# An fp32 encoder layer on one core: functions of finished products one product later in ScalarE's queue, matmuls of the means later in TensorE's

## The chip, the cores and the metric

The kernel runs on one core of one Trainium2 chip. The metric is the time on the device in microseconds (us), given as the median of several runs. One execution was also recorded by the hardware profiler, and every row shown here comes from that one.

## The reference

One layer of a two-branch encoder, in fp32, for two groups of tokens that share the weights: a prompt of 512 tokens and a sample of 1024, both 1024 wide. Cut to what matters:

```python
def conv_branch(a_val, a_glu, a_z, ...):
    h = a_val * jax.nn.sigmoid(a_glu)
    h = lax.conv_general_dilated(h, conv_w, ...) + conv_b      # depthwise, 31 taps
    h = layer_norm(h, ln_g, ln_b)
    h = jax.nn.silu(h) * jax.nn.silu(a_z)
    return h @ w_proj

def sgu_branch(u, v, b_z, ...):
    v = layer_norm(gelu(v), ln_g, ln_b)
    mixed = einsum("gpq,bnqgc->bnpgc", w_s, chunks(v)) + b_s
    return (gelu(u) * mixed * jax.nn.silu(b_z)) @ w_proj

def encoder_layer(x, c, ...):
    shift, scale, gate = split(silu(c) @ w_ada + b_ada)
    h = rms_norm(x, g_pre) * (1 + scale) + shift
    a_val, a_glu, a_z, u, v, b_z, g_a, g_b = split(h @ w_in)
    m = sigmoid(g_a) * conv_branch(...) + sigmoid(g_b) * sgu_branch(...)
    return x + gate * rms_norm(m @ w_out, g_post)
```

## The kernel before, in words

**Tiles.** Activations lie with the features on the 128 partitions and 512 tokens along a row. There are three such token tiles: the prompt `t0`, and the halves `sa` and `sb` of the sample. An fp32 product is made of three fp32r matmuls: each operand is split into a rounded part hi and a rest lo, and hi·hi, hi·lo and lo·hi are summed in a PSUM bank. A column step (128 output features of one tile, 8 blocks of 128 features deep) is 24 matmuls of 128x128 by 128x512, on the lines L449 to L451 and L472 to L474.

**Pairs.** The input projection of the sample is done two units of 128 output features at a time, by `pair` (L993), as a Strassen product: instead of eight half products it makes seven, of 12 matmuls each (L483 to L485): Xa, Ya, Xb, Zb, Xc, Zc, Xd. X, Y and Z are three banks; X runs on through four products, and between them ScalarE copies a snapshot of a bank into a work buffer (`snap`, L1014: p1 and u2 and u3 of X, s5 of Z), because the next product goes on adding to that bank. VectorE adds snapshots to banks (L1018 for C11, L1022 for C22, L1026 for C12). C11, C22, C12 and C21 are the four finished quarters, and `finish(what, st)` applies to each the function of its branch on ScalarE: `pair_func` (L1126 for quarters in a work buffer, L1131 for C21, which is still in the bank), `pair_mul` (L1148, L1153; then a product with a loaded tile on VectorE, L1158; the tile is asked for at L1142), or `pair_glu` (L1167 to L1173). There are 28 pairs in a row: 8 of glu, and 4 each of gB, um, hB, z and gA.

**What sets the order.** The program is written to the engines' queues by a planner that runs on the host. `steps` lists TensorE's steps; the loop at the end (L1715 on) goes through them. For each step `s` it writes, of the step before (`p`), `p.a1` to ScalarE; then it lets background generators (`bg`, mostly the convolution's taps at L403) put work on VectorE up to a time of the model (`fill`); then `p.d1` on VectorE, `p.a2` on ScalarE, `p.d2` on VectorE; then the matmuls of `s` on TensorE, and loads on SP's queue. Every engine works through its queue in the order in which it was written, so an instruction that waits holds up all that stand behind it on its engine.

**Means.** Two LayerNorms per token tile need a mean over the features, that is over partitions. `bcast_mean` (L324) makes hi and lo of a sum (ScalarE L320, VectorE L321), and two matmuls with a matrix of 1/1024 (L331, L332). These are not a step of their own: `pe_later(lag, cost, fn)` leaves them in a list, and the planner puts them into TensorE's queue at the first of its polls that is later than VectorE's model clock plus `lag`. `LAG` is 1.0. There are 12 such means in the program. `ln_gen` (L414) with `rstd_bcast` (L364) and `late_ln` (silu L1227, multiplication L1240, hi L1241, lo L1232) make the operand hA of a sample half from the convolution's result. The steps behind the pairs are, in this order as far as they matter here: post_B of both halves (product with sproj; VectorE takes the banks at L1292), post_A(sa) and then the output product `steps_o` of sa (ScalarE L610, VectorE L619, closing at L636 to L643), post_A(sb) (reads hA of sb; VectorE L580, L581), and steps_o of sb.

**Raw weights.** A weight block comes from HBM into `raw`, ScalarE makes hi (L247), and lo is made by VectorE (L259) or by ScalarE and a DMA of POOL (L250, L240).

Of the kernel before, what the change touches and what calls it, by code (L numbers as in the profile page):

```python
# [40 lines left out]
LAG = 1.0  # L41
# [39 lines left out]
def layer_kernel(ctx: ExitStack, tc, x_p, x_s, xt_p, xt_a, xt_b, par, w_blk, w_v, cproj, sproj, w_out, w_ada, w_gate, wsT, bs,  # L81
# [13 lines left out]
    V, S, PE, SP, GP = nc.vector, nc.scalar, nc.tensor, nc.sync, nc.gpsimd  # L95
# [107 lines left out]
    steps = []  # L203
# [70 lines left out]
    def fill(t_end, n=1000):  # L274
        while clk["dve"] < t_end and n > 0 and bg:
            i = 0
            while i < len(bg):
                r = next(bg[i], None)
                if r is None:
                    bg.pop(i)  # L280
                elif r == "wait":
                    i += 1
                else:
                    n -= 1
                    break
            else:
                clk["dve"] += 0.2
# [17 lines left out]
    def pe_later(lag, cost, fn):  # L305
        box = {}

        def go(now):
            box["b"] = fn()
            box["t"] = now  # L310
        pe_items.append((clk["dve"] + lag, cost, go))
        return box
# [12 lines left out]
    def bcast_mean(src):  # L325

        hi, lo = yield from parts(src)

        def go():
            b = bank()  # L330
            PE.matmul(b, lhsT=onemr, rhs=hi, start=True, stop=False)  # L331
            PE.matmul(b, lhsT=onemr, rhs=lo, start=False, stop=True)  # L332
            return b
        box = pe_later(LAG, 0.43, go)
        yield from ready(box)
        return box["b"]

# [651 lines left out]


    pairs = []

    def pair(src1, src2, finish):  # L993

        u1, u2 = Unit(src1, len(steps)), Unit(src2, len(steps))
        w = {}
        st = {}
# [5 lines left out]
        def prod(name, wt, i, opn, first, last, a1=None, d1=None, a2=None, need=None, act=0.6):  # L1003
            def mm():
                if first:
                    st[name] = bank()
                mm_prod(st[name], half(w[wt][0], i), half(w[wt][1], i), A[opn], first, last)
            s_ = add_step(Step(mm, a1, d1, a2, dur=PROD, need=need, act=act))
            return s_

        def snap(name, of):
            def a1():
                st[name] = wk()
                S.copy(st[name], st[of])  # L1014
            return a1
# [16 lines left out]
        mul = getattr(finish, "mul", None)  # L1032
        ask = getattr(finish, "ask", None)

        def times(*what):
            return (lambda: [mul(x) for x in what]) if mul else None

        prod("X", "a", 0, (0, 0), True, False, a1=snap("p1", "X"))
        prod("Y", "a", 1, (0, 1), True, True, d1=d_c11, a2=lambda: finish("C11", st), act=0.0)
        prod("X", "b", 0, "S2", False, False, a1=snap("u2", "X"), d1=times("C11"), need="S")  # L1040
        prod("Z", "b", 1, "S1", True, False, a1=snap("s5", "Z"))
        prod("X", "c", 0, "S3", False, False, a1=snap("u3", "X"), d1=d_c22, a2=lambda: finish("C22", st))
        prod("Z", "c", 1, "S4", False, True, d1=d_c12, a2=lambda: finish("C12", st), need="S4", act=0.0)
        steps[-1].d2 = times("C22")
        prod("X", "d", 0, (1, 1), False, True, a1=lambda: finish("C21", st),
             d1=times("C12", "C21") or (lambda: finish("end", st)))
        if ask:
            for i, what in ((1, ("C11",)), (3, ("C22",)), (4, ("C12", "C21"))):
                steps[i0 + i].extra = lambda what=what: [ask(x) for x in what]


# [654 lines left out]
    def events(s, kind):  # L1706
        for _, f in sorted(evs.pop((s, kind), []), key=lambda e: e[0]):
            f()

    for s in range(NH, n + 1):  # L1710
        p = steps[s - 1]
        st = steps[s] if s < n else None
        poll(clk["pe"])
        pe0 = clk["pe"]
        if st is not None:  # L1715
            if st.pre:
                clk["pe"] += st.pre()
            clk["pe"] += st.dur
        pe1 = clk["pe"]
        clk["act"] = max(clk["act"], pe0)  # L1720
        if p.a1:
            p.a1()
            clk["act"] += p.act
        events(s, "act")
        fill(pe0 + 0.5)
        if p.d1:
            dwait(pe0 + 0.7)
            p.d1()
        if p.a2:
            p.a2()  # L1730
            clk["act"] = max(clk["act"], clk["dve"]) + 0.6
        fill(pe1 - 1.5, 2)
        if p.d2:
            p.d2()
        events(s, "dve")
        if st is not None:
            t_need = clk["dve"]
            meet(st.need)
            if clk["dve"] > t_need and clk["dve"] > clk["pe"] - st.dur:
                clk["pe"] = clk["dve"] + st.dur  # L1740
                pe1 = clk["pe"]
            st.mm()
        load_some(s)
        if st is not None and st.extra:
            st.extra()
        fill(pe1 + 0.4)
        dwait(pe0 + 0.5)
# [68 lines left out]
```

## Time and profile before

| | us |
|---|---|
| median of 3 runs (1469.4 to 1471.98) | 1471.81 |
| the profiled execution | 1466.83 |
| its span, first to last instruction | 1464.9 |
| TensorE busy | 1432.5 (98%) |
| VectorE busy | 1129.0 (77%) |
| ScalarE busy | 742.3 (51%) |
| mean granted TensorE clock, as a share | 0.992 |

TensorE is the engine that is almost always busy. A matmul of 128x512 is listed with 0.39 us, but matmuls overlap: without a wait one starts every 0.227 us. A row of a timeline gives the start, the duration, the engine and line, the operation, what it writes and reads, and in brackets how long its engine had been idle before it and what released it. A gap between two starts on TensorE that is longer than 0.227 us is time lost to TensorE there.

### The profile page before, as it was taken

The page shows a single profiled execution, that of the slowest core. Times are in us where ns is not written, and L with a number is a line of the kernel's source. Part 1 is how long each engine was busy: PE and PEld are TensorE (multiplying, and loading weights), DVE is VectorE, ACT ScalarE, POOL GpSimd, SP SyncE. Part 2 cuts the span into 40 slices and gives each one's busy share as a digit, 9 for nine tenths or more (in the row PEclk, how much of TensorE's full clock was granted, in tenths as well). Part 3 has the DMA queues.
Part 4 walks back from the last instruction along what each step waited for, and adds up shares of the span by engine and source line. Part 5 has one row for each costly group of instructions (what it writes and reads, how often), then busy time and mean ns, then how long its engine had stood idle before and what let it go on. Part 6 is the DMA issues. An engine that isn't in the chain of part 4 may idle for free.

```text
span 1464.9 us, 17769 instructions
## 1 busy us (share of the span) xinstructions
PE 1432.5 (98%) x6332; PEld 1169.3 (80%) x6332; DVE 1129.0 (77%) x1596; ACT 742.3 (51%) x1064; POOL 186.2 (13%) x220
## 2 busy tenths in 40 slices
PE   8999999999999989999999999999999989999997
PEld 4688888888888878888888888877888867888886
DVE  6769999976356455867999898898999939587645
ACT  3532544553486454454545565555556545554442
POOL 0000111111111110011111111111111100000000
PEclk9999999999999999999999999999999999999999
DMA  9266787897999998967666878877977799878782
GB/s 342 79 215 182 198 201 166 203 256 181 279 266 244 284 263 272 281 168 201 155 158 166 209 194 242 255 211 218 256 192 191 194 307 276 265 222 237 211 269 72
DMA packets 120040, 321.68 MB, mean 220 GB/s; under 512 B 13328, under 2 KB 17040, under 8 KB 119184
## 3 DMA queue, kind: packets, MB, share of 16 engines
q1 hardware_dynamic: 88992, 229.85, 45.2%
q0 software_dynamic: 30960, 90.72, 33.7%
q8 instruction: 49, 0.80, 0.2%
q14 instruction: 39, 0.32, 0.1%
HBM read 182.10 MB, written 47.71 MB: 157 GB/s over the span
## 4 chain that ended last, share of the span: by engine, by line
PE 80%; DMA 11%; DVE 4%; issue 2%; ACT 2%; SPq 1%; DVEq 0%; ACTq 0%; POOLq 0%
PE b L451 11%; PE b L449 11%; PE b L450 11%; PE b L483 10%; PE b L484 10%; PE b L485 10%; PE b L473 4%; PE b L474 4%; PE b L472 4%; DMA lo<-raw 2%; DMA wk<-d 2%; PE b L568 1%; DMA raw<-in_w_blk_dram 1%; DMA raw<-in_sproj_dram 1%; DVE c L403 1%
## 5 line engine op out<-in xcount | busy, mean ns | idle before, releaser
L483 PE MATMUL b<-A,hi 128*128 128x512 f32 x784 | 306.8, 391 | 6.9 <-ACT wk L1014 6.9
L484 PE MATMUL b<-A,hi 128*128 128x512 f32 x784 | 305.8, 390 | 0.0
L485 PE MATMUL b<-A,lo 128*128 128x512 f32 x784 | 305.7, 390 | 0.0
L449 PE MATMUL b<-A,hi 128*128 128x512 f32 x776 | 303.7, 391 | 0.0
L451 PE MATMUL b<-A,lo 128*128 128x512 f32 x776 | 302.8, 390 | 0.2 <-DMA lo<-raw 0.2
L450 PE MATMUL b<-A,hi 128*128 128x512 f32 x776 | 302.8, 390 | 0.0
L403 DVE SCALAR_TENSOR_TENSOR c<-c,prm 128x1024 f32<-128x1024 f32 x240 | 297.3, 1278 | 0.6
L247 ACT CAST hi<-raw 128x1024 fp32r<-128x1024 f32 x145 | 152.0, 1048 | 262.4 <-DMA raw<-in_w_v_dram 61.7
L240 POOL DMA_DIRECT2D lo<-raw x131 | 113.4, 865 | 788.8 <-ACT lo L250 690.8
L483 PEld LDWEIGHTS b<-A,hi 128*128 128x128 f32 x784 | 147.6, 188 | 40.1 <-ACT wk L1014 9.7
L485 PEld LDWEIGHTS b<-A,lo 128*128 128x128 f32 x784 | 147.6, 188 | 30.5
L484 PEld LDWEIGHTS b<-A,hi 128*128 128x128 f32 x784 | 147.5, 188 | 30.6 <-DVE A L967 0.2
L451 PEld LDWEIGHTS b<-A,lo 128*128 128x128 f32 x776 | 146.1, 188 | 31.3 <-DMA lo<-raw 0.7
L449 PEld LDWEIGHTS b<-A,hi 128*128 128x128 f32 x776 | 146.1, 188 | 30.4 <-issue 0.2
L450 PEld LDWEIGHTS b<-A,hi 128*128 128x128 f32 x776 | 146.0, 188 | 30.5 <-issue 0.2
L403 DVE SCALAR_TENSOR_TENSOR S<-c,prm,S 128x512 f32<-128x512 f32 x240 | 162.6, 745 | 0.2
L473 PE MATMUL b<-lo,A 128*128 128x512 f32 x384 | 150.6, 392 | 5.0 <-DMA lo<-raw 5.0
L472 PE MATMUL b<-hi,A 128*128 128x512 f32 x384 | 150.8, 393 | 0.0
L474 PE MATMUL b<-hi,A 128*128 128x512 f32 x384 | 150.0, 391 | 0.0
L240 POOL DMA_DIRECT2D lo<-T x84 | 72.4, 862 | 456.7 <-ACT lo L1068 374.0
L1014 ACT COPY wk<-b 128x512 f32<-128x512 f32 x112 | 65.0, 585 | 121.2 <-PE b L485 117.5
L250 ACT ACTIVATE lo<-raw 128x1024 fp32r<-128x1024 f32 x103 | 108.7, 1055 | 0.0
(206 smaller groups left out, 1630.7 us busy)
## 6 DMA issues: line engine op xcount, KB each, us to landing
raw<-in_w_blk_dram SPq DMA_DIRECT2D x105, 512.0 KB, 5.6
lo<-raw POOLq DMA_DIRECT2D x103, 512.0 KB, 6.6
d<-wk SPq DMA_DIRECT2D x142, 256.0 KB, 3.7
wk<-d SPq DMA_DIRECT2D x116, 256.0 KB, 5.9
lo<-T POOLq DMA_DIRECT2D x28, 512.0 KB, 5.7
lo<-T POOLq DMA_DIRECT2D x56, 256.0 KB, 4.4
raw<-in_w_v_dram SPq DMA_DIRECT2D x24, 512.0 KB, 5.6
raw<-in_sproj_dram SPq DMA_DIRECT2D x24, 512.0 KB, 6.1
```

Source lines behind the costliest of these rows:

```text
L240: GP.dma_start(lo.bitcast(F32), src, accum_op=ALU.add)
L247: S.copy(u.hi, u.raw)
L403: lambda: V.scalar_tensor_tensor(acc, in0=win, scalar=wt, in1=acc, op0=ALU.mult, op1=ALU.add))
L449: PE.matmul(dst, lhsT=wh3[:, k, :], rhs=hi, start=(k == 0), stop=False)
L450: PE.matmul(dst, lhsT=wh3[:, k, :], rhs=lo, start=False, stop=False)
L451: PE.matmul(dst, lhsT=wl3[:, k, :], rhs=hi, start=False, stop=(k == NK - 1))
L472: PE.matmul(banks[i], lhsT=hi, rhs=wh3[:, kk, :], start=(k == 0), stop=False)
L473: PE.matmul(banks[i], lhsT=hi, rhs=wl3[:, kk, :], start=False, stop=False)
L474: PE.matmul(banks[i], lhsT=lo, rhs=wh3[:, kk, :], start=False, stop=(k == NK - 1))
L483: PE.matmul(dst, lhsT=wh3[:, k, :], rhs=hi, start=st, stop=False, skip_group_check=True)
L484: PE.matmul(dst, lhsT=wh3[:, k, :], rhs=lo, start=False, stop=False, skip_group_check=True)
L485: PE.matmul(dst, lhsT=wl3[:, k, :], rhs=hi, start=False, stop=sp, skip_group_check=True)
```

## The change

Two edits. In `bcast_mean` the matmuls of a mean are asked for `3 * LAG` after VectorE's model clock instead of `LAG`. Since they can enter only at the planner's polls (at and amid its steps), their place in TensorE's queue moves by 0, 12, 24, 36 or 48 matmuls. In `pair`, the function of C11, C22 and C12 is queued by `turn("act")` behind the snapshot that follows the next product; the multiplications (L1158) that belong to um and hB, and glu's last part, are kept for the step after and written after `fill`; and the loads that `pair_mul` asks for move from the steps 1, 3 and 4 of a pair to 2, 4 and 5. No instruction is added or removed on any engine.

```diff
@@ -331,7 +331,7 @@
             PE.matmul(b, lhsT=onemr, rhs=hi, start=True, stop=False)
             PE.matmul(b, lhsT=onemr, rhs=lo, start=False, stop=True)
             return b
-        box = pe_later(LAG, 0.43, go)
+        box = pe_later(3 * LAG, 0.43, go)
         yield from ready(box)
         return box["b"]
 
@@ -989,6 +989,12 @@
 
 
     pairs = []
+    late = {"act": [], "dve": []}
+
+    def turn(kind):
+        fns, late[kind] = late[kind], []
+        for f in fns:
+            f()
 
     def pair(src1, src2, finish):
 
@@ -1032,20 +1038,31 @@
         mul = getattr(finish, "mul", None)
         ask = getattr(finish, "ask", None)
 
-        def times(*what):
-            return (lambda: [mul(x) for x in what]) if mul else None
+        def after_next(what):
+
+            def act():
+                finish(what, st)
+                if mul:
+                    late["dve"].append(lambda: mul(what))
+            late["act"].append(act)
+
+        def c21():
+            finish("C21", st)
+            if mul:
+                late["dve"].append(lambda: mul("C21"))
+
+        def end():
+            late["dve"].append(lambda: finish("end", st))
 
         prod("X", "a", 0, (0, 0), True, False, a1=snap("p1", "X"))
-        prod("Y", "a", 1, (0, 1), True, True, d1=d_c11, a2=lambda: finish("C11", st), act=0.0)
-        prod("X", "b", 0, "S2", False, False, a1=snap("u2", "X"), d1=times("C11"), need="S")
+        prod("Y", "a", 1, (0, 1), True, True, d1=d_c11, a2=lambda: after_next("C11"), act=0.0)
+        prod("X", "b", 0, "S2", False, False, a1=snap("u2", "X"), need="S")
         prod("Z", "b", 1, "S1", True, False, a1=snap("s5", "Z"))
-        prod("X", "c", 0, "S3", False, False, a1=snap("u3", "X"), d1=d_c22, a2=lambda: finish("C22", st))
-        prod("Z", "c", 1, "S4", False, True, d1=d_c12, a2=lambda: finish("C12", st), need="S4", act=0.0)
-        steps[-1].d2 = times("C22")
-        prod("X", "d", 0, (1, 1), False, True, a1=lambda: finish("C21", st),
-             d1=times("C12", "C21") or (lambda: finish("end", st)))
+        prod("X", "c", 0, "S3", False, False, a1=snap("u3", "X"), d1=d_c22, a2=lambda: after_next("C22"))
+        prod("Z", "c", 1, "S4", False, True, d1=d_c12, a2=lambda: after_next("C12"), need="S4", act=0.0)
+        prod("X", "d", 0, (1, 1), False, True, a1=c21, d1=end)
         if ask:
-            for i, what in ((1, ("C11",)), (3, ("C22",)), (4, ("C12", "C21"))):
+            for i, what in ((2, ("C11",)), (4, ("C22",)), (5, ("C12", "C21"))):
                 steps[i0 + i].extra = lambda what=what: [ask(x) for x in what]
 
 
@@ -1718,9 +1735,11 @@
             clk["pe"] += st.dur
         pe1 = clk["pe"]
         clk["act"] = max(clk["act"], pe0)
+        muls, late["dve"] = late["dve"], []
         if p.a1:
             p.a1()
             clk["act"] += p.act
+        turn("act")
         events(s, "act")
         fill(pe0 + 0.5)
         if p.d1:
@@ -1730,6 +1749,8 @@
             p.a2()
             clk["act"] = max(clk["act"], clk["dve"]) + 0.6
         fill(pe1 - 1.5, 2)
+        for f in muls:
+            f()
         if p.d2:
             p.d2()
         events(s, "dve")
```

ScalarE's queue in a pair of gA. The names are tiles: `b` a PSUM bank, `wk` a work buffer, `raw` and `T` the weights; the first of the three copies is p1, and L1126 the sigmoid of C11. Before:

```order
L1014 COPY wk_6271<-b_6257 128x512
L1068 ACTIVATE lo_6274<-T34_6191 128x512
L1106 CAST hi_6273<-T34_6191 128x512
L1074 CAST hi_6294<-raw_6206 128x1024
L1126 ACTIVATE wk_6271<-wk_6271 128x512
L1014 COPY wk_6317<-b_6257 128x512
L1014 COPY wk_6333<-b_6319 128x512
L1068 ACTIVATE lo_6336<-T12_6301 128x1024
L1086 CAST hi_6335<-T12_6301 128x1024
```

The same place after, where L1014 is now L1020 and L1126 is L1143:

```order
L1020 COPY wk_6428<-b_6413 128x512
L1085 ACTIVATE lo_6431<-T34_6341 128x512
L1123 CAST hi_6430<-T34_6341 128x512
L1091 CAST hi_6450<-raw_6356 128x1024
L1020 COPY wk_6470<-b_6413 128x512
L1143 ACTIVATE wk_6428<-wk_6428 128x512
L1020 COPY wk_6490<-b_6475 128x512
L1085 ACTIVATE lo_6493<-T12_6454 128x1024
L1103 CAST hi_6492<-T12_6454 128x1024
```

The sigmoid of C11 stood ahead of the copies of u2 and of s5 and now stands between them. The function of C22 keeps its place behind u3, and the functions of C12 and C21 change places with each other.

TensorE's queue at the tenth mean, in the second stage of post_B. `onemr` is the matrix of 1/1024. Before, the mean stands between two column steps (`b_9753` is the column before it, `b_9798` the one after):

```order
L450 MATMUL b_9753<-A_9314,hi_9601 128x512
L451 MATMUL b_9753<-A_9314,lo_9602 128x512
L331 MATMUL b_9782<-wk_9748,onemr_90 128x512
L332 MATMUL b_9782<-wk_9749,onemr_90 128x512
L449 MATMUL b_9798<-A_9313,hi_9652 128x512
L450 MATMUL b_9798<-A_9313,hi_9652 128x512
```

After, it stands in the middle of the next column step, `b_9788`, 12 of whose matmuls are already ahead of it:

```order
L450 MATMUL b_9788<-A_9313,hi_9650 128x512
L451 MATMUL b_9788<-A_9313,lo_9651 128x512
L331 MATMUL b_9801<-wk_9748,onemr_90 128x512
L332 MATMUL b_9801<-wk_9749,onemr_90 128x512
L449 MATMUL b_9788<-A_9314,hi_9650 128x512
L450 MATMUL b_9788<-A_9314,hi_9650 128x512
```

The ninth mean, 86 matmuls earlier, stands in TensorE's queue exactly where it stood. The eleventh and twelfth stand 48 matmuls later.

VectorE's queue where steps_o of sa ends and post_A of sb begins. L1240 and L1232 (after: L1257 and L1249) are the multiplication and the lo of hA of sb, one of each for each of 8 blocks; L619 waits for the end of steps_o of sa. Before, all eight lo stand ahead of L619:

```order
L1240 TENSOR_TENSOR wk<-wk,c_10108 128x512
L1232 TENSOR_TENSOR A<-wk,A 128x512
L1240 TENSOR_TENSOR wk<-wk,c_10108 128x512
L1232 TENSOR_TENSOR A<-wk,A 128x512
L1240 TENSOR_TENSOR wk<-wk,c_10108 128x512
L1232 TENSOR_TENSOR A<-wk,A 128x512 x2
L619 TENSOR_TENSOR S<-b,G_9868 128x512 x4
L636 SCALAR_TENSOR_TENSOR ss<-q 128x4
L155 TENSOR_SCALAR r<-ss 128x4
```

After, four lo stand ahead of it:

```order
L1249 TENSOR_TENSOR A<-wk,A 128x512
L1257 TENSOR_TENSOR wk<-wk,c_10144 128x512
L1249 TENSOR_TENSOR A<-wk,A 128x512
L1257 TENSOR_TENSOR wk<-wk,c_10144 128x512
L619 TENSOR_TENSOR S<-b,G_9864 128x512 x4
L636 SCALAR_TENSOR_TENSOR ss<-q 128x4
```

and the other four behind it, behind the eleven small operations of L636 to L165 and a lo of weights (L259):

```order
L165 SCALAR_TENSOR_TENSOR r<-u,r 128x4
L259 TENSOR_TENSOR lo<-raw,hi 128x1024
L1249 TENSOR_TENSOR A<-wk,A 128x512
L1257 TENSOR_TENSOR wk<-wk,c_10144 128x512
L1249 TENSOR_TENSOR A<-wk,A 128x512
L1257 TENSOR_TENSOR wk<-wk,c_10144 128x512
L1249 TENSOR_TENSOR A<-wk,A 128x512 x2
L643 SCALAR_TENSOR_TENSOR S<-S,r 128x1024 x4
L580 TENSOR_TENSOR wk<-b,wk 128x512
```

## Rows read from the trace of the kernel before

**Rows 1.** The page, part 1: busy us (share of the span) and instructions of TensorE.
```profile
PE 1432.5 (98%) x6332; PEld 1169.3 (80%) x6332; DVE 1129.0 (77%) x1596; ACT 742.3 (51%) x1064; POOL 186.2 (13%) x220
```

**Rows 2.** Waits of TensorE (line waited for: us in total, times, longest).
```profile
PE b L483 <- ACT wk L1014: 6.9, 6, 2.1
PE b L473 <- DMA lo<-raw: 5.0, 4, 2.6
PE b L331 <- ACT wk L320: 4.1, 2, 2.6
```

**Rows 3.** Timeline of TensorE, one of the product stalls: start, duration, line, [idle before <-releaser].
```profile
1018.34 0.39 PE L485 MATMUL b<-A,lo 128*128 128x512 f32 x1
1020.53 0.50 PE L483 MATMUL b<-A,hi 128*128 128x512 f32 x1 [1.80 <-ACT wk L1014]
```

**Rows 4.** Timeline of ScalarE, the same stall.
```profile
1019.38 0.63 ACT L1148 ACTIVATE wk<-wk 128x512 f32<-128x512 f32 x1 [5.18 <-DVE wk L1018]
1019.92 1.06 ACT L1014 COPY wk<-b 128x512 f32<-128x512 f32 x2
```

**Rows 5.** Timeline of VectorE, the same product.
```profile
1013.27 0.69 DVE L1158 TENSOR_TENSOR wk<-wk 128x512 f32<-128x512 f32 x1 [1.33 <-DMA wk<-d]
...
1018.66 0.68 DVE L1018 TENSOR_TENSOR wk<-b,wk 128x512 f32<-128x512 f32 x1
```

**Rows 6.** Timeline of ScalarE, the sixth product stall.
```profile
1172.09 1.05 ACT L247 CAST hi<-raw 128x1024 fp32r<-128x1024 f32 x1 [3.45 <-DMA raw<-in_sproj_dram]
...
1174.01 0.61 ACT L1126 ACTIVATE wk<-wk 128x512 f32<-128x512 f32 x1
...
1175.55 1.06 ACT L1014 COPY wk<-b 128x512 f32<-128x512 f32 x2
```

**Rows 7.** Timeline of TensorE, the sixth product stall.
```profile
1173.66 0.39 PE L485 MATMUL b<-A,lo 128*128 128x512 f32 x1
1176.18 0.61 PE L483 MATMUL b<-A,hi 128*128 128x512 f32 x1 [2.13 <-ACT wk L1014]
```

**Rows 8.** Windows: us, busy us (count) per engine, granted clock, DMA share, GB/s.
```profile
1000.00:1050.00 50.00, 48.20 (x213) 39.59 (x212) 45.81 (x52) 27.73 (x45) 9.48 (x11) 1.00 0.81 220
1160.00:1180.00 20.00, 17.87 (x72) 14.30 (x72) 15.90 (x17) 12.48 (x21) 3.44 (x4) 0.91 1.04 293
1220.00:1240.00 20.00, 18.26 (x72) 14.38 (x72) 18.51 (x30) 9.43 (x13) 1.86 (x2) 0.91 0.79 203
```

**Rows 9.** Timeline of TensorE, the ninth and tenth means.
```profile
1207.82 0.50 PE L331 MATMUL b<-wk,onemr 128*128 128x512 f32 x1 [2.55 <-ACT wk L320]
...
1227.79 0.39 PE L451 MATMUL b<-A,lo 128*128 128x512 f32 x1
1229.70 0.50 PE L331 MATMUL b<-wk,onemr 128*128 128x512 f32 x1 [1.52 <-ACT wk L320]
1230.42 0.50 PE L332 MATMUL b<-wk,onemr 128*128 128x512 f32 x1 [0.22 <-DVE wk L321]
```

**Rows 10.** Timeline of VectorE, before the ninth and the tenth mean.
```profile
1200.92 1.22 DVE L259 TENSOR_TENSOR lo<-raw,hi 128x1024 fp32r<-128x1024 f32 x1 [15.26 <-ACT hi L247]
...
1206.38 0.69 DVE L423 TENSOR_TENSOR wk<-wk 128x512 f32<-128x512 f32 x1
...
1228.25 0.69 DVE L357 TENSOR_TENSOR wk<-wk 128x512 f32<-128x512 f32 x1
```

**Rows 11.** Timeline of VectorE, the second half's step to post_A.
```profile
1366.71 0.69 DVE L1232 TENSOR_TENSOR A<-wk,A 128x512 fp32r<-128x512 f32 x1 [2.07 <-ACT A L1241]
...
1370.38 0.69 DVE L619 TENSOR_TENSOR S<-b,G 128x512 f32<-128x512 f32 x1 [0.67 <-ACT wk L610]
1370.98 0.15 DVE L636 SCALAR_TENSOR_TENSOR ss<-q 128x4 f32<-128x4 f32 x1
...
1373.08 1.23 DVE L259 TENSOR_TENSOR lo<-raw,hi 128x1024 fp32r<-128x1024 f32 x1
```

**Rows 12.** Timeline of TensorE, the first post_A matmul of the second half.
```profile
1369.40 0.39 PE L449 MATMUL b<-A,hi 128*128 128x512 f32 x1
```

## The prediction

> **What bounds the kernel now.** I read the page first, then the waits of TensorE, then the timelines around each wait. TensorE is busy 1432.5 us of a span of 1464.9 [rows 1]; no instruction is added or removed, so only its gaps can change, some 32 us at most. Of these, the waits that the change can touch are six for a snapshot copy (L483 waiting for L1014, 6.9 us), two for a mean (L331 waiting for L320, 4.1 us) and four for weights (L473, 5.0 us) [rows 2]; the others lie at the start and in the outputs and keep their order. The reader is to see that nearly all the gain on offer is about 11 us of waits with what hangs on them, and that a gap also costs the restart.
>
> What a gap costs is seen at one of the product stalls: starts of 1018.34 and 1020.53 are 2.19 us apart where 0.227 is usual, 1.96 lost, though the wait is listed as 1.80 [rows 3]; the next matmul adds about 0.1. So I count 0.26 us for each gap beyond its listed wait. Some gaps cost the clock too: 1000 to 1050 us, with that gap in it, was granted 1.00, but 1160 to 1180 and 1220 to 1240 had 0.91 [rows 8]. Nine per cent of 20 us is 1.8 us lost to the lower of the two levels, 1.2 GHz.
>
> **The change, part by part.** *Five product stalls.* ScalarE's function of C11 waited 5.18 us for VectorE's addition, and the copies of u2 and s5 stood behind it: the addition starts 1018.66, the function 1019.38, the copies 1019.92, the matmul 1020.53 [rows 3 to 5]. Now u2 goes ahead of the function. Its bank was complete one product (12 x 0.227 = 2.72 us) before 1018.34, so it leaves the path. What is late next is s5, still behind the function: as timed here it would be copied from 1019.92 to 1020.5, and the product that needs it would start 2.72 us after the one that stalled, at 1018.34 + 0.23 + 2.72 = 1021.3. So there is 0.8 us to spare at the worst of the five. The six waits come to 6.9 us, the sixth alone to 2.1 [rows 2, 7]; 4.8 remain, and five times 0.26 make 6.1. But VectorE was late there because of its own loads (1.33 us at L1158 [rows 5]) and is busy 45.81 of 50 us [rows 8]: what TensorE gains, VectorE must make up out of some 4 us per 50, and otherwise s5 waits in u2's place. I take -5.0; the ends are -2.0 (only the two short ones of 0.5 us and a little of the others stay gone) and -6.1.
>
> *The sixth product stall* has another cause: ScalarE waits 3.45 us for raw weights until 1172.09, then works off L247, L250, the function at 1174.01, two L1269 and the copies at 1175.55 [rows 6]. The change takes only the function out of this row, 0.52 us by the step from 1174.01 to the next start. TensorE lost 2.52 - 0.23 = 2.29 us [rows 7] and 1.8 in the clock [rows 8]. The stall would be 1.8, about as long as the one that left the clock alone. I take 0.5 plus a good half of the clock: -1.5; ends 0 and -4.1.
>
> *The tenth mean.* TensorE lost 1.91 + 0.73 - 2 x 0.23 = 2.2 us in two gaps [rows 9] and 1.8 in the clock [rows 8]. ScalarE and VectorE were on the path: L357 at 1228.25 and what follows it [rows 10]. The mean's matmuls now stand 12 later in TensorE's queue, 2.72 us of work, which covers 2.2: -4.0, the restart's 0.1s being lost in rounding. The end on the other side is -2.2, if the clock falls there anyway.
>
> *The ninth mean* does not move in TensorE's queue: it waits 2.55 us for L320 [rows 9], behind a chain on VectorE that starts after L259, which itself had waited 15.26 us for weights [rows 10]. In the new order VectorE takes the first subtraction of that LayerNorm (L416) ahead of this L259, which frees the chain of its 1.22 us and of the weights; but the chain then hangs on tiles that come back from HBM, whose landing the trace shows only behind other waits. I take -1.5, between the whole of it (2.55, the second gap of 0.5 as at the tenth, the restart: -3.3) and +1.0, if those loads land later by about the time of that L259.
>
> *The other means.* The first eight belong to the prompt's and first half's norms; TensorE waited for none of them [rows 2]. They move by 0 to 48 matmuls, 48 x 0.227 = 10.9 us, and what depends on them has no wait listed on TensorE. What they shift on SP and ScalarE are the prompt's output weights and the first half's inputs, at the place of the L473 waits (5.0 us in four, the longest 2.6 [rows 2]). Single splits now stand ahead, others behind, so I cost it at 0, and from -4 to +4: most of these waits gone, or doubled less one.
>
> *The new wait.* The eleventh and twelfth means come 10.9 us later, and with them hA of the second half. Four of its eight lo now stand on VectorE behind the four L619, the small operations and an L259. In the trace the last L619 starts 1370.38, L636 0.60 later, L259 at 1373.08 [rows 11]; with its 1.22 [rows 10] the fifth lo would start 1374.3 and be there at 1374.95. TensorE begins post_A of this half at 1369.40 [rows 12]; three matmuls per block, the first lo of the fifth block is the 14th, at 1369.40 + 13 x 0.227 = 1372.35. That is 2.6 us of wait. Then each lo comes 1.2 us after the one before (a multiplication and a lo of 0.60 each, by the step from L619 to L636 [rows 11]) where TensorE works off a block in 0.68: 0.5 more at the sixth and the seventh, and three restarts of 0.1 or so. Together 3.8. With half of a clock loss of 1.8: +4.7; ends +2.5 and +6.5 (a longer chain and the whole clock). In the profile before the last lo was done 2 us ahead of the first of these matmuls, so nothing of it was paid.
>
> On the clock the rows say: a gap of 1.96 us left it whole, and a gap of 2.29 us, or two close to each other, went with 0.91 [rows 3, 7 to 9]. [...]
>
> **Sum.** -5.0 - 1.5 - 4.0 - 1.5 + 0 + 4.7 = -7.3 us, from the profiled execution's 1466.83 to 1459.5, a ratio of 0.995. The shown runs have a median of 1471.81, 5 us above the profiled one; the same ratio gives 1464.5.
>
> **Rivals.** *The gains shift on (no change).* VectorE has little room in the pairs, and the function of C11 still holds up s5, the functions of C12 and the multiplications come later, so that C11's stall may return one product on; and what TensorE gains in the pairs it may wait out at the ninth mean, whose chain starts from weights and loads and not from TensorE. For it: the idle of 15.26 us at L259 [rows 10], which TensorE cannot shorten. Against it: 0.8 us are spare at s5. The product stalls then give 2 at most and the sixth and the ninth 0; with -4.0 for the tenth and +4.7 it is -1.3: 1470.5.
>
> *Slower: hA of the second half comes far too late.* The price of the new wait was worked out with the first four lo in time. If the later means also hold up VectorE (it waits for each one's result in its queue) the chain to the first lo slips up to the 10.9 us by which the matmuls moved; then all eight lo or the closing of sa's output stand between. Of 10.9 us, the 2 us by which the last lo was early [rows 11, 12] and half of the rest may be made up on VectorE: 4.5 more than the 4.7, with the clock whole 0.9 more, 10.1 in all. It decides the sign once the wait exceeds 12.0 us, the sum of the gains as I took them, and with the gains of the first rival, 6.0, at half that: -6.0 + 10.1 = +4.1, 1476. For it: 48 matmuls are two whole column steps, and VectorE's order there has become denser. Against it: in the new order the first four lo still stand ahead of L619.
>
> *All of it goes.* The five stalls -6.1, sixth -4.1, ninth -3.3, tenth -4.0, new wait +2.5: -15.0, 1456.8. For it: each is plain in a row. Against it: the sixth and the ninth stalls wait for weights.
>
> *It doesn't do what it says for the means.* Of the two means that TensorE waits for, one stays where it was; if the planner's lag helps the tenth no better (its chain starts from the ninth), the tenth's 4.0 is lost: -3.3, 1468.5.
>
> **Chances.** The forecast 0.47; all of it 0.12; no change 0.18; the tenth not helped 0.08; slower 0.15. Under 0.2%, 2.9 us, a difference cannot be told from none here. Faster: nearly all of the forecast, all of the full gain, and a part of the tenth's case: 0.62. Slower: that case and a little of the no-change one: 0.16. The rest, 0.22, the same. The likeliest case alone spans 1459 to 1469; the range that holds 8 in 10 reaches from the full gain's 1456 to 1475, short of the slower case's 1476.
>
> **What would show it.** In the profile after, L483 waiting for L1014 falls from six waits to two or fewer, and L1014 for u2 starts under 1 us after its bank is complete. L331 keeps one wait of 1 to 2.6 us and loses the other. L450, waiting for VectorE's lo (now L1249), appears once with 2 to 3 us near the start of post_A of the second half. The granted clock of the tenth's window goes to 1.00. I would be wrong if snapshot waits reappear on the copy of s5, if the post_A wait exceeds 6 us, if the waits for weights at the prompt's end grow by more than 4 us, or if VectorE's waits for the loaded tiles at its multiplications (now L1175) grow well beyond what they were.

## The result, and the profile after

The changed kernel took 1477.06 us (median of 6 runs, 1475.42 to 1481.52), the kernel before in the same comparison 1469.47 us (6 runs). The measured ratio is 1.0058 (the ratios here are not simply those of the two medians), 95% interval 1.004 to 1.0076: slower by 0.6%. The forecast was 0.995. The profiled execution of after took 1475.42 us with a span of 1473.5, 8.6 us more than the span of before; it is the lowest of the six.

TensorE carries out the same 6332 matmuls in both, and but for the means and one small mix (L568) in the same order. So the start of the n-th matmul in either trace shows where the time went between these two executions:

| matmul no. | before, us | after, us | after − before | what lies in the stretch that ends here |
|---|---|---|---|---|
| 1633 | 379.71 | 378.87 | -0.8 | the start |
| 1681 | 390.68 | 394.50 | +3.8 | weights late in the prompt: +4.7 |
| 2209 | 511.11 | 514.61 | +3.5 | |
| 2545 | 594.49 | 602.21 | +7.7 | the prompt's end: +4.2 |
| 3985 | 907.00 | 914.04 | +7.0 | pairs: one old stall gone, -0.7 |
| 4081 | 928.76 | 942.57 | +13.8 | pairs: two new stalls, +6.8 |
| 5185 | 1188.79 | 1192.80 | +4.0 | pairs: the other old stalls gone, -9.8 |
| 5281 | 1213.94 | 1219.86 | +5.9 | the ninth mean: +1.9 |
| 5377 | 1239.64 | 1241.68 | +2.0 | the tenth mean: -3.9 |
| 6001 | 1381.18 | 1389.80 | +8.6 | post_A of the second half: +6.6 |
| 6332 | 1456.21 | 1464.83 | +8.6 | the last one |

The waits of TensorE after, to be held against [rows 2]; lines have moved, and L1020 is what L1014 was, L1249 what L1232 was:

```profile
PE b L473 <- DMA lo<-raw: 8.6, 4, 4.4
PE b L483 <- ACT wk L1020: 4.6, 2, 3.2
PE b L450 <- DVE A L1249: 4.0, 1, 4.0
PE b L331 <- ACT wk L320: 3.0, 1, 3.0
PE b L451 <- DMA lo<-raw: 2.8, 1, 2.8
```

Snapshots fell from six waits to two, as forecast, but one of those is 3.2 us; one of the two means is gone, as forecast; L450 waits for the lo of hA, as forecast, with 4.0. What I had charged nothing for are the weights: L473 went from 5.0 to 8.6, and L451 went from 0.2 to 2.8.

**Weights in the prompt.** SP's queue, before:

```profile
358.13 0.33 SPq L522 DMA_DIRECT2D d<-wk  x1
...
359.47 2.02 SPq L146 DMA_DIRECT2D c<-in_w_gate_dram  x2
361.61 20.93 SPq L223 DMA_DIRECT2D raw<-in_w_blk_dram  x6
```

and after:

```profile
363.25 0.33 SPq L522 DMA_DIRECT2D d<-wk  x1
...
364.58 0.91 SPq L146 DMA_DIRECT2D c<-in_w_gate_dram  x2
365.93 24.39 SPq L223 DMA_DIRECT2D raw<-in_w_blk_dram  x6
```

The first row is the put of a half of the gate vector, the second the weights of its other half, and behind them stand weight blocks of the projection (six in this stretch). In the order the put had hardly moved (one weight block that stood behind it now stands ahead); but the put has to wait for VectorE, and VectorE for a mean. VectorE before, then VectorE and ScalarE in after:

```profile
356.69 0.69 DVE L1680 SCALAR_TENSOR_TENSOR wk<-b,bg 128x512 f32<-128x512 f32 x1 [3.33 <-PE b L332]
```

```profile
361.81 0.69 DVE L1697 SCALAR_TENSOR_TENSOR wk<-b,bg 128x512 f32<-128x512 f32 x1 [5.21 <-PE b L332]
...
375.02 0.88 DVE L1689 TENSOR_SCALAR wk<-c,sc 128x512 f32<-128x512 f32 x2 [11.80 <-DMA c<-in_w_gate_dram]
```
```profile
379.95 1.05 ACT L247 CAST hi<-raw 128x1024 fp32r<-128x1024 f32 x1 [12.06 <-DMA raw<-in_w_blk_dram]
```

The mean stands 24 matmuls later, and VectorE waited 5.21 us for L332, its second matmul (3.33 before). So the put, and all that stands behind it on SP, came 5.1 us later. The block whose hi starts at 379.95, the first behind the put, reached ScalarE 5.4 us later than in before, where its row is this:

```profile
374.55 1.04 ACT L247 CAST hi<-raw 128x1024 fp32r<-128x1024 f32 x1
```

On TensorE an L451 started at 386.85, 3.22 us after the matmul ahead of it (383.63). These means belong to `gate_gen`, which calls `bcast_mean` twice for each half of the gate vector, once for either group of tokens: four of the twelve. Of the other eight, six are the convolution's LayerNorm, two for each token tile, and two are the RMS norms of the sample halves' inputs. So it isn't two LayerNorms per tile that have such means, as the text ahead of the prediction says, and the first eight are not norms alone, as the prediction had it.

**The prompt's end.** ScalarE's waits for w_out before and after:

```profile
ACT hi L247 <- DMA raw<-in_w_out_dram: 4.9, 2, 3.7
```
```profile
ACT hi L247 <- DMA raw<-in_w_out_dram: 15.5, 3, 9.9
```

The largest gap on TensorE there grew from 3.0 us to 4.8 (528.21 to 532.99). How much of this the change causes is not shown. Eight of the kernels below (pair_only, c11_only, pair_ask, mul_late, b_1_3, b_6_3, b13_ask and b63_ask) have the order of before on every engine up to matmul 2545, and in their profiles the same stretch took between 1.2 us less and 4.7 us more than in the profile of before. In c11_only, the one with 4.7, the waits for w_out were these:

```profile
ACT hi L247 <- DMA raw<-in_w_out_dram: 11.8, 4, 5.4
```

In the five profiles with the prompt's other means later (after, lag_only, gate_lag1, sb_lag1 and ask_early) it took 3.6 to 5.6 us more. So later means may cost something there, but the profile of before lost less at this place than seven of those eight, and 4.2 is probably too much for them. The gate vector's stretch is clearer: from matmul 1633 to 1681 those eight, and gate_lag1, show 0.0, and the four others with these means late show 1.6 to 4.7.

**The two new product stalls.** On VectorE what led to both, then ScalarE and TensorE at the second (L400 is the convolution's first tap on a tile loaded from HBM, L1032 the sum of C12, L1175 the multiplication by a loaded tile, L1024 the sum of C11, L1165 its function):

```profile
921.10 0.82 DVE L400 TENSOR_SCALAR c<-c,prm 128x1024 f32<-128x1024 f32 x1 [3.18 <-DMA c<-d]
921.83 0.69 DVE L1032 TENSOR_TENSOR wk<-b,wk 128x512 f32<-128x512 f32 x1
...
928.11 0.69 DVE L1175 TENSOR_TENSOR wk<-wk 128x512 f32<-128x512 f32 x1 [3.20 <-DMA wk<-d]
...
933.52 0.68 DVE L1024 TENSOR_TENSOR wk<-b,wk 128x512 f32<-128x512 f32 x1
```
```profile
934.23 0.63 ACT L1165 ACTIVATE wk<-wk 128x512 f32<-128x512 f32 x1 [6.88 <-DVE wk L1024]
934.77 0.57 ACT L1020 COPY wk<-b 128x512 f32<-128x512 f32 x1
```
```profile
935.39 0.50 PE L483 MATMUL b<-A,hi 128*128 128x512 f32 x1 [3.22 <-ACT wk L1020]
```

The first stall, from 921.97 to 923.71 on TensorE, comes from the convolution's tile: C12's sum stands behind it, C12's function behind the sum, and the next pair's p1 behind the function. The second is the old stall one copy further on: the multiplication waits 3.20 us for its tile, the sum of C11 is late, C11's function waits 6.88 us, and behind it stands the copy, now of s5 alone. [rows 3 to 5] showed the same with u2 in that place. But the wait for a loaded tile by itself doesn't give a stall of this size. In pair_only, whose VectorE has the same order here, the same multiplication waited longer,

```profile
918.17 0.69 DVE L1175 TENSOR_TENSOR wk<-wk 128x512 f32<-128x512 f32 x1 [4.32 <-DMA wk<-d]
```

and TensorE did not stall; there the convolution's tile had landed 4.4 us after its request and VectorE hardly waited for it, while in after it took 7.5 us. b_1_3 and b_6_3 are like pair_only, with 5.1 and 4.8 us at the multiplication, and have gaps of 1.2 and 1.4 us on TensorE where after has 3.6. gate_lag1 and sb_lag1 have both waits (2.93 and 2.68, 3.18 and 3.04 us) and gaps of 3.1 and 3.4. Why the convolution's tile lands late in these three kernels, all with late means, is not shown.

**The ninth mean.** VectorE and ScalarE, to be held against [rows 10]:

```profile
1194.58 0.69 DVE L416 TENSOR_TENSOR wk<-c 128x512 f32<-128x512 f32 x1 [5.73 <-DMA c<-d]
1204.71 1.23 DVE L259 TENSOR_TENSOR lo<-raw,hi 128x1024 fp32r<-128x1024 f32 x1 [9.44 <-ACT hi L247]
1205.86 0.69 DVE L418 TENSOR_TENSOR wk<-c 128x512 f32<-128x512 f32 x1
```
```profile
1203.63 1.05 ACT L247 CAST hi<-raw 128x1024 fp32r<-128x1024 f32 x1 [11.73 <-DMA raw<-in_sproj_dram]
```

L416 did go ahead of L259, by ten us; but L418, its successor, still stands behind it, and L259 behind a hi whose weights came from HBM at 1203.63. TensorE came 4.0 us later than before (table, matmul 5185), the mean 4.5 us, so that the wait was 3.0 us (2.55 in [rows 9]). By an estimate, 1.2 of the 1.9 us are the clock: behind this gap stood six starts at 0.427 in place of 0.227 us, behind that of before none.

**Post_A of the second half.** VectorE, to be held against [rows 11]:

```profile
1371.79 2.85 DVE L619 TENSOR_TENSOR S<-b,G 128x512 f32<-128x512 f32 x4 [1.62 <-ACT wk L610]
...
1377.78 0.69 DVE L1249 TENSOR_TENSOR A<-wk,A 128x512 fp32r<-128x512 f32 x1
```

The four L619 waited 1.62 us for ScalarE, which now had hi and silu of hA to do as well, so that the fifth lo came 1.4 us later against TensorE's first matmul of the step (1371.44) than I had it. The clock of three of these stretches:

```profile
380.00:390.00 10.00, 7.17 (x25) 5.49 (x24) 5.88 (x9) 9.60 (x12) 2.60 (x3) 0.84 0.78 163
930.00:940.00 10.00, 6.78 (x23) 5.13 (x22) 9.97 (x13) 3.58 (x5) 0.86 (x1) 0.83 0.50 136
1220.00:1240.00 20.00, 20.00 (x90) 16.52 (x89) 18.03 (x28) 12.73 (x19) 2.85 (x3) 1.00 0.79 237
1370.00:1390.00 20.00, 16.02 (x61) 12.61 (x60) 17.11 (x32) 9.33 (x17) 0.86 (x1) 0.83 0.45 133
```

The tenth mean's window is whole again at 1.00 (0.91 in [rows 8]); the three new long stalls have 0.83 or 0.84.

### The profile page after: what moved, and what is told of

Read it like the earlier page. It is cut to its first block, busy times and chain, and to the rows that moved or that the text cites. A ratio compares the mean times of both kernels' runs of the same rounds, so it can differ in the third digit from the quotient of the medians.

```text
span 1473.5 us, 17769 instructions
## 1 busy us (share of the span) xinstructions
PE 1434.1 (97%) x6332; PEld 1172.1 (80%) x6332; DVE 1129.1 (77%) x1596; ACT 742.4 (50%) x1064; POOL 186.2 (13%) x220
## 4 chain that ended last, share of the span: by engine, by line
PE 83%; DMA 9%; DVE 4%; issue 2%; ACT 1%; SPq 1%; DVEq 0%; POOL 0%; POOLq 0%; ACTq 0%
PE b L451 11%; PE b L450 11%; PE b L449 11%; PE b L483 11%; PE b L485 11%; PE b L484 11%; PE b L473 4%; PE b L472 4%; PE b L474 4%; DMA wk<-d 2%; DMA raw<-in_w_blk_dram 1%; PE b L568 1%; DMA lo<-raw 1%; DMA raw<-in_w_v_dram 1%; DMA raw<-in_w_out_dram 1%
## 5 line engine op out<-in xcount | busy, mean ns | idle before, releaser
L483 PE MATMUL b<-A,hi 128*128 128x512 f32 x784 | 306.2, 391 | 4.6 <-ACT wk L1020 4.6
L450 PE MATMUL b<-A,hi 128*128 128x512 f32 x776 | 304.3, 392 | 4.0 <-DVE A L1249 4.0
L451 PE MATMUL b<-A,lo 128*128 128x512 f32 x776 | 304.4, 392 | 2.8 <-DMA lo<-raw 2.8
L483 PEld LDWEIGHTS b<-A,hi 128*128 128x128 f32 x784 | 147.6, 188 | 36.0 <-ACT wk L1020 5.4
L450 PEld LDWEIGHTS b<-A,hi 128*128 128x128 f32 x776 | 146.9, 189 | 35.4 <-DVE A L1249 4.9
L451 PEld LDWEIGHTS b<-A,lo 128*128 128x128 f32 x776 | 146.9, 189 | 33.8 <-DMA lo<-raw 3.2
L473 PE MATMUL b<-lo,A 128*128 128x512 f32 x384 | 150.7, 392 | 8.6 <-DMA lo<-raw 8.6
L1020 ACT COPY wk<-b 128x512 f32<-128x512 f32 x112 | 65.4, 584 | 124.0 <-PE b L485 115.1
```

The source lines that it names most:

```text
L450: PE.matmul(dst, lhsT=wh3[:, k, :], rhs=lo, start=False, stop=False)
L451: PE.matmul(dst, lhsT=wl3[:, k, :], rhs=hi, start=False, stop=(k == NK - 1))
L473: PE.matmul(banks[i], lhsT=hi, rhs=wl3[:, kk, :], start=False, stop=False)
L483: PE.matmul(dst, lhsT=wh3[:, k, :], rhs=hi, start=st, stop=False, skip_group_check=True)
```

## The experiments

Each was timed against the kernel before on the same chip. A profile is of one execution, and the runs of the kernel before spread from 1464.3 to 1478.8 us over these comparisons: a profile tells where TensorE waited in that execution, the ratio what the edit was worth.

**The means alone (lag_only).** The edit to the kernel before:

```diff
-        box = pe_later(LAG, 0.43, go)
+        box = pe_later(3 * LAG, 0.43, go)
```

> The kernel before with the one edit 3*LAG; pairs as before. Theory A (the means carry the loss): TensorE's pace after against before gave +4.7 us near 385 us, +3.9 at the prompt's end, +6.6 where post_A of the second half begins, -3.9 at the tenth mean and +1.9 at the ninth; all of that should be here and the six product stalls too: +9 to +14 us, ratio 1.006 to 1.010. Theory B (the pairs carry it, means harmless): 0 to +2 us, ratio 1.000 to 1.001.

Ratio 1.0057 (1.0039 to 1.0076). Theory A holds, though a little under its range (its interval reaches into it). The trace has the waits of after and the old product stalls together:

```profile
PE b L473 <- DMA lo<-raw: 7.4, 4, 2.5
PE b L483 <- ACT wk L1014: 6.1, 5, 2.5
PE b L450 <- DVE A L1232: 4.0, 1, 4.0
```

**The pairs alone (pair_only).** The kernel after, with the line above undone.

> The kernel after with the means at LAG again; only the pair edits stay. Theory A: TensorE's pace gained 3.7 us over the pairs, so -2 to -6 us, ratio 0.996 to 0.9985, with one or two stalls left where VectorE waits for the tiles that pair_mul loads. Theory B: +4 to +9 us, ratio 1.003 to 1.006.

Ratio 0.9944 (0.9923 to 0.9964). The pairs gain, and more than theory A expected. TensorE's waits there:

```profile
PE b L331 <- ACT wk L320: 5.2, 2, 3.6
...
PE b L483 <- ACT wk L1020: 1.3, 1, 1.3
```

One product stall is left. The ninth mean waits 3.6 us instead of 2.6: TensorE was 5.6 us earlier than before at matmul 5185, and the mean came 3.6 us earlier. So what it waits for follows TensorE in good part, but not wholly. The two edits don't add up: 1.0057 and 0.9944 would give 1.000 together, after has 1.0058. Most of what is lost between them, some 8 us, are the two new stalls: from matmul 3985 to 4081 after lost 6.8 us, pair_only 0.3 and lag_only 0.0.

**LAG for the gate vector's means (gate_lag1).** The kernel after, with

```diff
-                b = yield from bcast_mean(ts_[g])
+                b = yield from bcast_mean(ts_[g], LAG)
```

(the second argument being the lag, 3*LAG elsewhere).

> The kernel after with LAG for the four means of the gate vector (gate_gen) alone. Theory A (the later means delay the put of the gate vector, which holds SP's queue with weights behind it): the put on SP comes near 358 us again instead of 363, the L451 stall near 385 us falls from 3.2 us to under 1, 4 to 5 us come back there, and part of the 3.9 at the prompt's end: 4 to 8 us less than after. Rival (the weights are late because the DMA engines are saturated there, whatever SP does): the stall stays at 2 us or more, 0 to 1 us less than after.

Ratio 1.0018 (1.0003 to 1.0034), some 6 us less than after. The put and the weights on SP:

```profile
357.93 0.33 SPq L522 DMA_DIRECT2D d<-wk  x1
...
359.27 2.00 SPq L146 DMA_DIRECT2D c<-in_w_gate_dram  x2
361.39 21.91 SPq L223 DMA_DIRECT2D raw<-in_w_blk_dram  x6
```

So the put is back at 357.93. The stall of 3.2 us is gone; 24 matmuls ahead, where before has a gap of 0.6 us between two starts, stands one of 1.5, more than the 1 us expected. But the eight kernels with the prompt of before have 1.0 to 1.9 there as well, so against them the later means cost some 1 us less than the table's 4.7. Of the prompt's end little came back: TensorE's pace still loses 3.6 us there against before. The rival's answer (0 to 1 us less) didn't come: the same loads, with the put early, are in time.

**LAG for the second half's LayerNorm (sb_lag1).** The kernel after, where `late_ln` calls:

```diff
-        yield from ln_gen(t, t.acc)
+        yield from ln_gen(t, t.acc, LAG if t is sb else 3 * LAG)
```

(the third argument being the lag of both its means).

> The kernel after with LAG for the two means of the second half's LayerNorm alone; in VectorE's queue all eight lo then stand ahead of the four L619 again. Theory A: the wait of L450 for L1249 (4.0 us, with the slow clock behind it 6.6) is gone: 6 to 7 us less than after. Rival (TensorE would wait there for something else, the weights or the output step): 0 to 3 us less, with another wait near 1375 us.

Ratio 1.0002 (0.9985 to 1.0019), some 8 us less than after. The wait of L450 is gone and nothing stands in its place. The two means still stood 36 and 24 matmuls later than before; that was harmless, 48 was not, because with 48 four lo fall behind the L619.

**C11's function alone (c11_only).** The kernel before, with

```diff
-        ... a2=lambda: finish("C11", st), act=0.0)
+        ... a2=lambda: late["act"].append(lambda: finish("C11", st)), act=0.0)
```

and `turn("act")` behind `p.a1()`.

> The kernel before with one of the edits: the function of C11 is queued behind the next snapshot; C22, C12, the multiplications, the loads they ask for and the means are as before. Theory: all product stalls were copies behind C11's function, so this alone gives what the pair edits gave (ratio 0.9944): 0.993 to 0.997, with no L483 wait above 1.5 us. Rival: the moved multiplications and loads gave a good part of it: 0.997 to 1.000.

Ratio 1.0035 (1.0017 to 1.0054): my theory fell, and the rival, which allowed for no loss, fell short. Eight stalls where there were six:

```profile
PE b L483 <- ACT wk L1020: 9.5, 8, 4.6
```
```profile
DVE wk L1164 <- DMA wk<-d: 15.9, 13, 5.3
```

The profiled execution is the highest of the twelve (1479.72 us, the median 1474.72), so its waits may be longer than usual. VectorE's multiplications (L1164 in this kernel) wait 15.9 us for tiles (7.0 before, when it was L1158); why, when neither they nor their loads have moved, is not shown. At 929.08 the gap was 5.0 us: VectorE had waited 4.12 us for a tile of the convolution (c<-d), and C11's sum behind it was late enough to hold up s5 too. Taking u2 out of the way is worth nothing when VectorE is later than the product that it was given.

**Loads asked for earlier (ask_early).** The kernel after, with

```diff
-            for i, what in ((2, ("C11",)), (4, ("C22",)), (5, ("C12", "C21"))):
+            for i, what in ((1, ("C11",)), (3, ("C22",)), (4, ("C12", "C21"))):
```

> The kernel after, with pair_mul's loads asked for at the steps 1, 3 and 4 of a pair again. Theory: the two product stalls near 922 and 932 us (they cost 1.5 and 5.2 us of TensorE's pace) come from multiplications that wait on VectorE for tiles asked for too late; they vanish, VectorE's waits at L1175 for wk<-d fall from 15 us to under 8, and 4 to 7 us come back: ratio 1.001 to 1.003. Rival: VectorE is late there because the convolution's tiles (c<-d) land late: the stalls stay, ratio 1.005 to 1.007.

Ratio 0.999 (0.9974 to 1.0005), 10 us less than after, more than expected, with the means still late. No wait of L483 is left at all:

```profile
PE b L473 <- DMA lo<-raw: 8.1, 4, 4.4
PE b L450 <- DVE A L1249: 4.0, 1, 4.0
PE b L331 <- ACT wk L320: 2.9, 1, 2.9
```

and the idle time ahead of the 32 multiplications went from 15.4 to 9.7 us:

```profile
L1175 DVE TENSOR_TENSOR wk<-wk 128x512 f32<-128x512 f32 x32 | 21.3, 687 | 15.4 <-DMA wk<-d 15.1 <-ACT wk L1020 0.2
```
```profile
L1175 DVE TENSOR_TENSOR wk<-wk 128x512 f32<-128x512 f32 x32 | 21.4, 689 | 9.7 <-DMA wk<-d 5.4 <-issue 4.2
```

Of that, 5.4 us are listed as waits for tiles. But the 4.2 listed as issue are nearly all one wait, and its tile landed at 922.63, so it is a wait for a tile as well:

```profile
922.71 1.29 DVE L1175 TENSOR_TENSOR wk<-wk 128x512 f32<-128x512 f32 x2 [4.25 <-issue]
```

So the waits for tiles fell by a third and not below 8, and this one cost TensorE nothing. The stalls vanished as the theory has it, but their cause is not shown: the convolution's tile landed 4.2 us after its request here (7.5 in after), and VectorE didn't wait for it either, so the rival's cause was gone together with the theory's. Of the 9.0 us by which this profile is shorter than that of after, 6.8 are the two stalls; 3.1 lie at the gate vector's stretch, which the edit doesn't touch.

**The same with the means early (pair_ask):** the kernel after with this edit and the means at LAG.

> The pair edits with the means at LAG, and pair_mul's loads asked for at the steps 1, 3 and 4 again: the multiplications then stand two products behind their loads instead of one. Theory: VectorE no longer waits for tiles in um and hB, C11's sum is on time, and no product stall is left: 2 to 5 us less than pair_only, ratio 0.991 to 0.993. Rival: with the means early those waits cost TensorE little (one stall of 1.7 us in pair_only): 0.9935 to 0.9955.

Ratio 0.9928 (0.9907 to 0.9949) against pair_only's 0.9944: the intervals overlap, so a gain from asking earlier is shown where the means are late and is left open where they are early. No product stall is left here either.

**Multiplications late, functions early (mul_late).** As the one above, with

```diff
-            def act():
-                finish(what, st)
-                if mul:
-                    late["dve"].append(lambda: mul(what))
-            late["act"].append(act)
+            finish(what, st)
+            if mul:
+                late["act"].append(lambda: late["dve"].append(lambda: mul(what)))
```

> As pair_ask, but ScalarE's functions stand where they stood before (C11's ahead of u2's and s5's copies); only the multiplications and glu's last part are later. Theory D (the waits for tiles make VectorE late, and the order on ScalarE only passes it on): ratio within 0.002 of pair_ask. Theory S (the place of C11's function ahead of the copies is what stalls TensorE): three or more of the L483 stalls of before remain, ratio 0.996 to 0.999.

Ratio 0.9966 (0.9949 to 0.9982), 0.004 from pair_ask, and there are five stalls, three of them at products that stalled before:

```profile
PE b L483 <- ACT wk L1020: 6.6, 5, 2.7
```

Theory S has it: the place on ScalarE counts. But the later multiplications alone give about half of the gain (0.9966, where both together give 0.9928), and c11_only, C11's function alone, loses: its new place pays only if VectorE is on time too. The whole gain needs both halves.

**The tenth mean alone later (b_1_3).** Pair edits, LAG everywhere but there:

```diff
+        yield from ln_gen(t, t.acc, *((1 * LAG, 3 * LAG) if t is sa else ()))
```

(the lags of its first and its second mean).

> The pair edits, LAG for all means but the second mean of the first half's LayerNorm (the tenth), which has 3*LAG. Theory: the pair edits' 0.9944 and the tenth's stall (2.0 and 0.7 us and the slow clock, 4 us) go together: ratio 0.991 to 0.993. Rival: the ninth and what follows give it back: 0.994 to 0.996.

Ratio 0.9929 (0.9902 to 0.9956): at the rim of the theory's range, and not told apart from pair_only by the interval. The trace shows the tenth's stall gone: from matmul 5281 to 5377 TensorE gained 3.9 us on before, in pair_only it lost 0.1.

**And the ninth (b_6_3):** `6 * LAG` in place of `1 * LAG`.

> As b_1_3, and the ninth mean gets 6*LAG, which puts it 12 matmuls later and the tenth 24. Theory: the ninth's stall (4.0 us) does not hang on TensorE, so 12 matmuls (2.7 us) put ahead of it are 2 to 3 us less than b_1_3: 0.989 to 0.991. Rival: the chain behind it (tenth mean, hA of the first half) comes late by as much: same as b_1_3 or up to 2 us more.

Ratio 0.9936 (0.9914 to 0.9957): the rival's answer. Both kernels also exist with the loads asked for early, as b13_ask and b63_ask.

> pair_ask with 3*LAG for the tenth mean alone. Theory: the tenth's stall goes as it went in b_1_3, 2 to 4 us less than pair_ask: ratio 0.989 to 0.991. Rival: what the ninth mean waits for does not hang on TensorE, so that gains ahead of it are waited out there: within 0.001 of pair_ask.

> b13_ask with 6*LAG for the ninth mean, which puts it 12 matmuls later. Theory: the ninth's wait of some 3.5 us shrinks by 2.7: 0.987 to 0.990. Rival (in b_6_3 an L451 stall of 2.9 us for weights stood a few us behind it): the weights of post_B are as late as the mean, so TensorE waits for them instead: same as b13_ask or 1 to 2 us more.

Ratios 0.9911 (0.9889 to 0.9933) and 0.991 (0.9888 to 0.9932), 1458.51 and 1458.28 us: the two fastest kernels of this study, and level. b13_ask lies 0.0017 under pair_ask, between its theory and its rival, with overlapping intervals, so the time tells neither; b63_ask gives its rival's answer. Why the ninth's place gives nothing, in the second of them:

```profile
1200.39 0.49 PE L331 MATMUL b<-wk,onemr 128*128 128x512 f32 x1 [0.29 <-ACT wk L320]
...
1204.56 0.79 PE L451 MATMUL b<-A,lo 128*128 128x512 f32 x1 [2.47 <-DMA lo<-raw]
```

The mean's wait shrank from 3.6 us in b13_ask to 0.3, and 4 us further on L451 waits 2.5 for a lo of weights: the weights and the mean had been late together.

## Why the prediction was wrong

The sum said -7.3 us and the two profiles differ by +8.6. By the table, 7.7 of the 15.9 us between lie ahead of the pairs, 2.8 in the pairs, 3.4 at the ninth mean, 1.9 at the new wait and 0.1 at the tenth.

- *The step that failed is "the other means", costed at 0.* The means alone made the kernel 0.6% slower (lag_only). The prediction took the first eight for norms on which nothing on TensorE waits. Four are the gate vector's, whose put blocks SP's queue 5.1 us longer with the weights behind it: +4.7 us, and setting these four back takes 0.4% off. The rule I broke is that a moved step counts with its DMAs: I followed the matmul on TensorE and the order on SP, in which the put had hardly moved, but not the time of what it waits for. At the prompt's end the profiles show another +4.2, but executions with the same order differ there by as much; whether the prompt's other means cost anything there, and which, stays open.
- *The five product stalls*, -5.0: these stalls went, as the mechanism had it, for the whole -6.1, but that was paid back by two new ones: 5.2 us on s5, the copy I had named as next, with 0.8 us to spare, and 1.5 us near 922 us on the next pair's p1, which stands behind C12's function, a place I had not priced. I had counted VectorE as late by what it was late before. It was later by two things that my sum didn't charge: the multiplications, whose loads are asked for one step later, waited 15.1 us in place of 7.0, and ahead of C12's sum VectorE waited 3.18 us for a tile of the convolution. Without the second wait (pair_only, b_1_3 and b_6_3) the stall is small or absent; which of the two ask_early cured isn't shown. So the return of the copy of s5, and the longer waits at L1175, were two of the prediction's own signs of being wrong.
- *The sixth stall*, -1.5, went whole (its 4.1 are among the 9.8): too small. *The tenth mean*, -4.0, came to -3.9, and b_1_3 shows it by itself. Part of the match is luck: c11_only, where this mean stands as before, has -3.9 there too, after it lost 6.9 us at its ninth mean.
- *The ninth mean*, -1.5, was +1.9: only L416 was freed from L259; I read the first subtraction of the chain and not its second. My first rival said that TensorE would wait out there what it had won. In after it had won nothing by then; in pair_only it had won 5.6 us, and this stretch took 3.2 of them back.
- *The new wait*, +4.7, was 6.6: mechanism and place right (without it, in sb_lag1, the stretch lost 0.0), but the first wait was 4.0 us where I had 2.6 (ScalarE held up the L619), and the clock did fall: ten starts behind it were 0.427 us apart. The parts of its price also add up to 3.9 and not to 3.8.
- *The rival "slower"* put the whole loss at post_A; that its 1476 lies near the 1477 measured is luck. The sign followed from several places: with any one of the three put right, the gate vector, post_A or the late loads, the ratio is within 0.2% of 1 (1.0018, 1.0002, 0.999).

## What to carry to other kernels

When a matmul is moved back, follow its result to the next DMA that is issued from an in-order queue, and count what stands behind that DMA; an unmoved row in the order can still be five us later. When an instruction is queued later, leave the request of its inputs where it was: with the means late that was worth 10 us here. Taking a copy from behind a wait moves the stall to the next copy unless the wait itself gets shorter, and a place where several late things meet (a mean and its weights) gives nothing until all are early. Two profiles are two executions: before a difference between them is put down to a change, see how much the same stretch differs where nothing was changed.

## What the runs showed of the hardware

Behind the gaps of 3.2, 3.6 and 4.4 us on TensorE in after, six to ten starts lay 0.427 us apart, the lower level of 1.2 GHz, and the granted clock of the windows around them was 0.83 or 0.84. The gap of 1.7 us (921.97 to 923.71) was followed by starts at the usual 0.227. The length of the gap doesn't settle it: the one of 2.6 us at 589.72 had no slow start behind it either, nor had one of 3.07 us in mul_late (1175.51 to 1178.58), and the sixth product stall of before with 2.5 us had (0.91 in [rows 8]). The prediction's reading, by which gaps above some 2 us went with the lower clock, had left out the ninth mean of [rows 9]: from 1204.88 to 1207.82 are 2.94 us, and the window around it was granted 1.00 (the number before the last two):

```profile
1200.00:1215.00 15.00, 12.23 (x53) 9.49 (x52) 13.22 (x20) 8.62 (x13) 0.86 (x1) 1.00 1.04 359
```

I had taken the clock at half its price for the new wait; each of the gaps above 3 us in after paid it.
